# Operand sums of a two-level Strassen feed-forward moved beside the projections, and attention probabilities per head pair

## The chip, the cores and the metric

The kernel runs on one core of a Trainium2 chip. TensorE multiplies matrices, VectorE, ScalarE and GpSimd (DVE, ACT and POOL in the profile) work element by element, and SyncE (SP) issues nearly all transfers, from one queue, in order. The metric is the time of one execution on the device in microseconds.

## The reference, cut to what matters

One decoder layer on 2048 tokens of width 1024: a modulated RMSNorm, a combined projection, sliding-window attention beside a state-space scan, an output projection, a second modulated RMSNorm and a gated feed-forward of width 2816.

```python
h = modulate(rmsnorm(x, norm1_w), shift1, scale1)
x = x + gate1 * hybrid_mixer(h, ...)      # attention and SSD heads, then @ w_out
h = modulate(rmsnorm(x, norm2_w), shift2, scale2)
x = x + gate2 * swiglu(h, w_gate_up, w_down)
return rmsnorm(x, final_norm_w)

# in the attention, per head, over a band of 256 keys
m = maximum(max(scores), sink)
p = exp(scores - m)
probs = p / (sum(p) + exp(sink - m))
# swiglu
g, u = split(h @ w_gate_up, 2)
out = (silu(g) * u) @ w_down
```

## The kernel before

**Tiling.** Tokens are held in four blocks of 512 columns; features lie on the 128 partitions. Every f32 product is made from split operands: a rounded upper half (`hi`, written by ScalarE) and the rest (`lo`, by VectorE or GpSimd), three products per pair (`mm3`, lines 275 to 277; `product`, lines 918 to 920).

**Stages.** Blocks 0 to 3 go through norm, queries, keys and values, `convolved` (16 steps: eight column groups in two halves), and `gated` (eight steps). Attention and state-space work of earlier blocks is interleaved as "sides": after every step of the main stage `tick` (line 1224) advances the sides by a ratio, counts down entries of `pending`, and starts those that have reached zero. `norm_ahead(b, at)` (line 1266) puts the four parts of the norm of block b there: squares and their sum at once, then the root (`rstd`, a product with ones, line 290), the spread over partitions (line 319) and the modulated operands (`modulated`, lines 324 to 327) at the ticks given.

**Order of the work.** Up to line 1342 TensorE's order is the one written in the program. The other engines, and TensorE later on, are ordered by a planner that simulates the program and takes, on each engine, the earliest traced instruction that is ready. SP's queue gets its order in the same way.

**The feed-forward's first product.** Two blocks of tokens make a group, s = 0 for blocks 0 and 1, s = 1 for blocks 2 and 3. The gate and up products of a group use a Strassen-Winograd form (`quad`, 22 of them per group): seven products in place of eight, with sums of operands. With h[i, j] the half i of the features of block j of the group, the operands are b11 and b21 (from block one alone), b22 (from block two alone), t1 = h01 - h00, t3 = h11 - h01, t2 = h00 + t3 and t4 = h10 - t2, each made for four K tiles, shifts added. `scaled` (lines 862 to 870) loads a tile of the residual from DRAM (`mid`, L868) and multiplies it by the norm's scale and root (L869). `shifted` (L874, L875) and `kept` (L879, L880) write the two halves of an operand. `operands_first` makes b11 and b21, `operands_between` t1, `operands_last` b22, t3, t2, t4. For s = 0 the first two run beside `convolved(3)` (lines 1333 to 1338), the last is emitted in one piece after the first product of the first quad (line 1356). For s = 1 `last_operands` (line 1391) runs as a side of `down(1)`, between first, last after it. A first quad takes its products K tile by K tile (`fresh`).

**Attention.** Per tile of 128 tokens, `scores` runs twice (four heads each), then `probabilities` for all eight heads: eight exponentials with sums (L650), the denominators (L651 to L653), eight scalings (L656). The transposes and products with the values of the tile before (`held`, lines 558 to 566; `transposed`, L662 to L666; `values`) come after each pair.

**Buffers and tail.** `tmp` has eight tiles (256 KB each) for all uses; `staged` four (z, q and kv on their way to DRAM); `extra` gives working tiles to the state-space side of blocks 0 and 1. In `down(3)` the last norm's root uses ScalarE's square root (`quick_root`, L307); line 1001 issues a square root with no operand from the data ahead of it.

## Time and profile before

| | us |
|---|---|
| median of three runs | 2375.27 |
| lowest, highest | 2369.06, 2376.70 |
| the profiled execution | 2371.23 |
| its span, first to last instruction | 2369.5 |
| TensorE busy | 2245.6 |
| VectorE busy | 1463.7 |
| GpSimd busy | 1240.4 |
| ScalarE busy | 962.0 |

A span stands on the time line from the first instruction on. An engine's busy time counts its compute instructions; idle time in front of an instruction is put down to what released it, and a line like "PE d L290 <- POOL acc L285" reads: TensorE, writing d at line 290, waited for GpSimd's write of acc at line 285. PEclk is the granted clock of TensorE as a share of 2.4 GHz.

### The profile page before, as it was taken

The numbers are of one execution on the slowest core, as the hardware profiler recorded it, in microseconds if no ns is written. First come the engines' busy times: TensorE is split into PE (matmuls) and PEld (weight loads), VectorE is DVE, ScalarE is ACT, GpSimd is POOL, SyncE is SP. The second block draws the span as 40 slices with busy tenths as digits, with TensorE's granted clock in tenths as the row PEclk, the third lists the DMA queues.
The fourth block names the chain that finished last, engine by engine and source line by source line (L and its number), as shares of the span: only waits on it lengthen the run. The fifth ranks groups of instructions, "written<-read, shape, count | busy, mean of one in ns | idle before, by whom it ended". The sixth has DMA issues, their size and how long they took to land.

```text
span 2369.5 us, 33207 instructions
## 1 busy us (share of the span) xinstructions
PE 2245.6 (95%) x11292; PEld 1861.3 (79%) x11292; DVE 1463.7 (62%) x2549; ACT 962.0 (41%) x2002; POOL 1240.4 (52%) x1227
## 2 busy tenths in 40 slices
PE   6788989999999899999999999988999999999998
PEld 5578788788878688887888788866788888888787
DVE  8887975673465865667755453499654445454544
ACT  4454543654255545333333332334333333343332
POOL 2756433453222764787875432437766666653441
PEclk9899999999999899999999999999999999999999
DMA  8898977677885322332234865575322222263452
GB/s 294 287 332 302 308 252 245 229 249 261 279 266 158 117 82 78 103 107 87 92 98 150 268 214 177 165 260 161 135 92 81 85 83 82 81 221 103 130 181 63
DMA packets 249065, 412.22 MB, mean 174 GB/s; under 512 B 22464, under 2 KB 68544, under 8 KB 248896
## 3 DMA queue, kind: packets, MB, share of 16 engines
q1 hardware_dynamic: 248320, 409.58, 52.8%
q8 instruction: 89, 1.46, 0.3%
q14 instruction: 80, 0.66, 0.1%
q10 hardware_dynamic: 576, 0.52, 0.1%
HBM read 315.58 MB, written 94.44 MB: 173 GB/s over the span
## 4 chain that ended last, share of the span: by engine, by line
PE 43%; DVE 4%; DMA 1%; issue 1%; POOL 1%; ACT 0%; SPq 0%; DVEq 0%; POOLq 0%; ACTq 0%
PE d L275 5%; PE d L276 5%; PE d L277 5%; PE d L918 5%; PE d L920 5%; PE d L919 5%; PE am L920 1%; PE am L918 1%; PE am L919 1%; PE sm L920 1%; PE sm L918 1%; PE sm L919 1%; DVE t L869 1%; PE am L275 1%; PE am L277 1%
## 5 line engine op out<-in xcount | busy, mean ns | idle before, releaser
L919 PE MATMUL d<-b,w 128*128 128x512 f32 x924 | 367.5, 398 | 3.0 <-POOL b L880 2.9
L918 PE MATMUL d<-b,w 128*128 128x512 f32 x924 | 366.2, 400 | 3.6 <-ACT b L879 1.6
L920 PE MATMUL d<-b,w 128*128 128x512 f32 x924 | 366.1, 398 | 2.8 <-DVE w L850 2.8
L849 ACT ACTIVATE w<-raw 128x512 fp32r<-128x512 f32 x308 | 193.1, 630 | 432.6 <-PE d L277 218.2
L275 PE MATMUL d<-a,w 128*128 128x512 f32 (+1 forms) x720 | 282.9, 396 | 17.4 <-DVE x L1029 13.3
L276 PE MATMUL d<-a,w 128*128 128x512 f32 (+1 forms) x720 | 280.6, 390 | 1.9 <-DVE a L844 1.9
L277 PE MATMUL d<-a,w 128*128 128x512 f32 (+1 forms) x720 | 282.0, 392 | 0.0
L850 DVE TENSOR_TENSOR w<-raw,w 128x512 fp32r<-128x512 f32 x220 | 211.2, 962 | 73.1 <-ACT w L849 69.7
L850 POOL TENSOR_TENSOR w<-raw,w 128x512 fp32r<-128x512 f32 x88 | 121.4, 1380 | 221.8 <-ACT w L849 203.1
L1029 DVE SCALAR_TENSOR_TENSOR x<-d,mod,x 128x512 f32<-128x512 f32 (+1 forms) x182 | 131.0, 724 | 170.9 <-PE d L277 168.0
L919 PEld LDWEIGHTS d<-b,w 128*128 128x128 f32 x924 | 175.0, 189 | 43.2 <-POOL b L880 4.3
L918 PEld LDWEIGHTS d<-b,w 128*128 128x128 f32 x924 | 174.4, 189 | 43.4 <-ACT b L879 2.6
L920 PEld LDWEIGHTS d<-b,w 128*128 128x128 f32 x924 | 174.4, 189 | 43.4 <-DVE w L850 3.3
L850 POOL TENSOR_TENSOR w<-s,w 128x512 fp32r<-128x512 f32 x132 | 190.9, 1448 | 23.2 <-ACT w L849 22.3
L849 ACT ACTIVATE w<-s 128x512 fp32r<-128x512 f32 x176 | 111.0, 632 | 210.5 <-PE d L920 157.0
L275 PE MATMUL d<-w,hl 128*128 128x256 f32 (+1 forms) x592 | 175.7, 297 | 4.4 <-ACT hl L326 2.3
L275 PEld LDWEIGHTS d<-a,w 128*128 128x128 f32 x720 | 135.9, 189 | 53.9 <-DVE x L1029 9.1
L276 PE MATMUL d<-w,hl 128*128 128x256 f32 (+1 forms) x592 | 170.9, 289 | 0.0
L277 PE MATMUL d<-w,hl 128*128 128x256 f32 (+1 forms) x592 | 170.6, 288 | 0.0
L276 PEld LDWEIGHTS d<-a,w 128*128 128x128 f32 x720 | 136.3, 189 | 33.5 <-DVE a L844 3.1
L277 PEld LDWEIGHTS d<-a,w 128*128 128x128 f32 x720 | 135.7, 188 | 30.8 <-issue 0.5
L934 POOL TENSOR_TENSOR s<-raw,s 128x512 f32<-128x512 f32 x44 | 58.6, 1331 | 186.6 <-DVE w L850 112.6
(387 smaller groups left out, 5457.3 us busy)
## 6 DMA issues: line engine op xcount, KB each, us to landing
raw<-in_wgu_dram SPq DMA_DIRECT2D x176, 256.0 KB, 2.7
raw<-in_wd_dram SPq DMA_DIRECT2D x176, 256.0 KB, 2.7
w<-w_x SPq DMA_DIRECT2D x48, 512.0 KB, 5.3
w<-w_o SPq DMA_DIRECT2D x48, 512.0 KB, 4.6
act<-t SPq DMA_DIRECT2D x88, 256.0 KB, 2.1
t<-act SPq DMA_DIRECT2D x88, 256.0 KB, 4.5
t<-in_xT_dram SPq DMA_DIRECT2D x80, 256.0 KB, 4.4
aw<-in_wada_dram SPq DMA_DIRECT2D x64, 256.0 KB, 4.2
```

The costliest lines, as they stand in the source:

```text
L275: nc.tensor.matmul(out, ahi, bhi, start=first, stop=False)
L276: nc.tensor.matmul(out, ahi, blo, start=False, stop=False)
L277: mm3.last = nc.tensor.matmul(out, alo, bhi, start=False, stop=last)
L849: nc.scalar.activation(hi, x, AF.Copy)
L850: eng.tensor_tensor(lo, x, hi.bitcast(F32), ALU.subtract)
L869: nc.vector.scalar_tensor_tensor(x, x, scl2[:, d:d + 1], bc[j], ALU.mult, ALU.mult)
L918: nc.tensor.matmul(out, ahi, bhi, start=first and k == 0, stop=False, skip_group_check=True)
L919: nc.tensor.matmul(out, ahi, blo, start=False, stop=False, skip_group_check=True)
L920: mm3.last = nc.tensor.matmul(out, alo, bhi, start=False, stop=k == 3, skip_group_check=True)
L934: nc.gpsimd.tensor_tensor(s4, a12, s2, ALU.subtract)
L1029: nc.vector.scalar_tensor_tensor(x, ps, gate2[:, c:c + 1], x, ALU.mult, ALU.add)
```

## The change

It has five parts. First, for s = 0 the sums t3, t2, t4 and the scaled h11 are computed beside `convolved(3)` and `gated(3)` (`sums_ahead`), stored to DRAM (`raw_d`) and loaded again after the first quad's first product (`operands_kept`), where only the halves are written; the lower half of t2 goes to VectorE, those of t3 and t4 stay on GpSimd. `operands_first` and `operands_between` move to earlier steps. Second, `probabilities` runs once per pair, for four heads. Third, for s = 1 the separate pass for t1 is gone, t1 comes out of the pass of `operands_last`, with one more yield. Fourth, the ticks of the norms of blocks 1 and 3 are later. Fifth, the square root without data is tied to an operand of the fourth group of `down(3)`; `staged` has six tiles, the extra working tiles are nine.

```diff
-    common, extra = tiles(sb, M1, M2, M4), tiles(xp, 3, 10, 4)
+    common, extra = tiles(sb, M1, M2, M4), tiles(xp, 3, 9, 4)
...
-        return small([P, 256], "so", 4, pool=ip)
+        return small([P, 256], "so", 6, pool=ip)
...
-                if pair_of:
-                    probabilities(st, sms, slots)
-                    if t + 1 < NT:
-                        nxt = load(t + 1)
+                probabilities(st, sms, slots, pair_of)
+                if pair_of and t + 1 < NT:
+                    nxt = load(t + 1)
...
-    def probabilities(st, sms, slots):
-        mx, nm, den, es = (st[:, i, :] for i in range(4))
+    def probabilities(st, sms, slots, pair_of):
+        heads = range(4 * pair_of, 4 * pair_of + 4)
+        mx, nm, den, es = (st[:, i, 4 * pair_of:4 * pair_of + 4] for i in range(4))
...
+    raw_d = [[dr.tile([P, T], F32, name=f"raw_{n}{k}") for n in ("b22", "t3", "t2", "t4")] for k in range(4)]
+
+    def sums_ahead(s, bc):
+
+        for k in range(4):
+            h = scaled(s, k, bc, ((1, 1), (0, 1), (0, 0), (1, 0)))
+            t3, t2, t4 = h[0, 1], h[0, 0], h[1, 0]
+            nc.vector.scalar_tensor_tensor(t3, h[1, 1], dsh[:, k:k + 1], h[0, 1], ALU.add, ALU.subtract)
+            nc.vector.scalar_tensor_tensor(t2, h[0, 0], shift_of(k, 0), t3, ALU.add, ALU.add)
+            nc.vector.scalar_tensor_tensor(t4, h[1, 0], shift_of(k, 1), t2, ALU.add, ALU.subtract)
+            for to, x in zip(raw_d[k], (h[1, 1], t3, t2, t4)):
+                nc.sync.dma_start(to, x)
+            yield
+
+    def operands_kept(ops):
+        for k in range(4):
+            got = []
+            for n, src in zip(("t2", "t3", "b22", "t4"), (2, 1, 0, 3)):
+                x = tmp()
+                scaled.last = nc.sync.dma_start(x, raw_d[k][src])
+                got.append((n, x))
+            for n, x in got:
+                if n == "b22":
+                    shifted(ops[n][k], x, shift_of(k, 1))
+                else:
+                    kept(ops[n][k], x, nc.vector if n == "t2" else nc.gpsimd)
...
-            t3, t2, t4 = h[0, 1], h[0, 0], h[1, 0]
+            t3, t1, t2, t4 = h[1, 1], h[0, 1], h[0, 0], h[1, 0]
             nc.vector.scalar_tensor_tensor(t3, h[1, 1], dsh[:, k:k + 1], h[0, 1], ALU.add, ALU.subtract)
             kept(ops["t3"][k], t3)
+            nc.vector.tensor_tensor(t1, h[0, 1], h[0, 0], ALU.subtract)
+            kept(ops["t1"][k], t1)
+            yield
...
-            nc.scalar.activation(small([P, 1], "first_root", 1, pool=x_pool), ident[:, 0:1], AF.Sqrt)
+            first_root = small([P, 1], "first_root", 1, pool=x_pool)
...
+                    if at_group == 3 and c == 0 and b == NB - 1:
+                        nc.scalar.activation(first_root, act[0][0][:, 0:1].bitcast(F32), AF.Sqrt, scale=0.0)
...
-                nxt = norm_ahead(1, (11, 14, 15))
+                nxt = norm_ahead(1, (12, 18, 19))
...
-        nxt = norm_ahead(3, (6, 12, 22))
+        nxt = norm_ahead(3, (10, 15, 22))
...
-            if i == 8:
+            if i == 6:
+                drain(firsts)
                 bcs.append(spread(y_of[1], bc=side_bank(3)))
                 firsts = operands_between(0, ops, bcs)
-            if i % 2:
+            if i == 12:
+                drain(firsts)
+                firsts = sums_ahead(0, bcs)
+            if i < 4 or 6 <= i < 14 and i % 2 == 0 or i >= 12 and i % 2:
+                next(firsts, None)
+        for i in beside(gated(3, h), 0.5):
+            if i in (1, 3):
                 next(firsts, None)
         drain(firsts)
-        run(gated(3, h), 0.5)
...
-    drain(operands_last(0, ops, bcs))
+    operands_kept(ops)
...
-        yield from operands_between(1, ops, bcs)
         yield from operands_last(1, ops, bcs)
```

## Rows read from the trace of the kernel before

**Rows 1.** The page: span, and busy time of TensorE with its share and instructions.
```profile
span 2369.5 us, 33207 instructions
...
PE 2245.6 (95%) x11292; PEld 1861.3 (79%) x11292; DVE 1463.7 (62%) x2549; ACT 962.0 (41%) x2002; POOL 1240.4 (52%) x1227
```

**Rows 2.** Stretches of 20 us: length, busy PE, PEld, DVE, ACT, POOL, PEclk, DMA, GB/s.
```profile
420.00:440.00 20.00, 14.74 (x72) 12.15 (x71) 13.07 (x38) 7.30 (x16) 11.50 (x23) 0.83 0.50 172
...
760.00:780.00 20.00, 15.58 (x86) 12.46 (x85) 15.49 (x23) 13.80 (x33) 13.17 (x10) 1.00 0.48 150
780.00:800.00 20.00, 13.93 (x59) 10.65 (x58) 19.40 (x31) 8.31 (x16) 11.33 (x9) 0.73 0.57 166
800.00:820.00 20.00, 18.22 (x83) 13.81 (x81) 17.59 (x29) 13.59 (x39) 15.42 (x11) 0.93 0.22 80
```

**Rows 3.** What TensorE waited for, whole run: us in total, times, longest us.
```profile
PE d L275 <- DVE x L1029: 13.3, 9, 3.9
PE am L275 <- DVE m L666: 11.8, 6, 3.5
...
PE d L290 <- POOL acc L285: 5.3, 1, 5.3
...
PE d L319 <- DVE t L317: 2.8, 1, 2.8
```

**Rows 4.** Stretches of 5 us around the root of block 3.
```profile
425.00:430.00 5.00, 1.19 (x6) 1.20 (x6) 2.78 (x3) 2.53 (x4) 4.58 (x11) 0.75 0.48 154
430.00:435.00 5.00, 5.00 (x20) 4.47 (x20) 3.42 (x10) 1.54 (x3) 3.16 (x7) 0.57 0.03 11
```

**Rows 5.** VectorE's group of 1535 to 1650 us, and stretches there.
```profile
L869 DVE SCALAR_TENSOR_TENSOR t<-t,scl,bc 128x512 f32<-128x512 f32 x8 | 5.7, 738 | 0.0
...
1580.00:1600.00 20.00, 16.06 (x65) 11.64 (x64) 20.00 (x29) 6.56 (x12) 9.50 (x7) 1.00 0.71 221
...
1640.00:1660.00 20.00, 15.62 (x61) 12.12 (x60) 16.11 (x18) 9.19 (x16) 15.37 (x11) 0.91 0.36 101
```

**Rows 6.** Groups of VectorE, 760 to 812 us, by form: busy us, mean ns, idle before.
```profile
L869 DVE SCALAR_TENSOR_TENSOR t<-t,scl,sm 128x512 f32<-128x512 f32 x8 | 5.9, 736 | 0.5 <-DMA t<-mid 0.5
L869 DVE SCALAR_TENSOR_TENSOR t<-t,scl,st 128x512 f32<-128x512 f32 x8 | 5.8, 740 | 3.6 <-DMA t<-mid 3.5
L907 DVE SCALAR_TENSOR_TENSOR t<-t,mod 128x512 f32<-128x512 f32 x4 | 4.6, 1148 | 0.0
```

**Rows 7.** Groups of GpSimd, 755 to 812 us, by form.
```profile
L880 POOL TENSOR_TENSOR b<-t,b 128x512 fp32r<-128x512 f32 x12 | 17.0, 1422 | 6.8 <-ACT b L879 6.8
...
L616 POOL TENSOR_TENSOR v_ring<-m,v_ring 128x128 fp32r<-128x128 f32 x2 | 0.9, 464 | 25.9 <-ACT v_ring L615 25.9
```

**Rows 8.** Timeline of GpSimd, 755 to 812 us: start, us, what.
```profile
766.54 1.30 POOL L928 TENSOR_TENSOR s<-raw 128x512 f32<-128x512 f32 x1
...
808.83 2.51 POOL L880 TENSOR_TENSOR b<-t,b 128x512 fp32r<-128x512 f32 x2
```

**Rows 9.** Stretches of 20 us beside conv and gates of block 3.
```profile
720.00:740.00 20.00, 20.00 (x124) 17.34 (x124) 8.96 (x19) 8.74 (x17) 7.07 (x11) 0.97 0.63 178
740.00:760.00 20.00, 20.00 (x175) 19.73 (x175) 6.64 (x19) 8.10 (x25) 0.21 (x1) 1.00 0.22 80
```

**Rows 10.** The page: a store of one tile, KB, median us from issue to landing.
```profile
act<-t SPq DMA_DIRECT2D x88, 256.0 KB, 2.1
```

**Rows 11.** ScalarE's timeline behind eight exponentials; TensorE's wait in 180 to 200.
```profile
179.78 0.36 ACT L665 ACTIVATE m<-am 128x256 fp32r<-128x256 f32 x1
...
PE am L275 <- DVE m L666: 2.0, 1, 2.0
```

**Rows 12.** Timeline of the tail.
```profile
2352.98 1.28 ACT L307 ACT_TABLE_LOAD   x1
...
2354.51 0.17 DVE L308 RECIPROCAL qr<-qr 128x2 f32<-128x2 f32 x1 [2.02 <-ACT qr L307]
```

**Rows 13.** What SP's queue waited for, 640 to 830 us.
```profile
SPq L498 <- DVE so L497: 19.0, 5, 10.4
```

More of the change, by code (lines that the diff above doesn't have):

```diff
@@ L641, in scores @@
         return sms
-    def probabilities(st, sms, slots):
-        mx, nm, den, es = (st[:, i, :] for i in range(4))
+    def probabilities(st, sms, slots, pair_of):
+        heads = range(4 * pair_of, 4 * pair_of + 4)
+        mx, nm, den, es = (st[:, i, 4 * pair_of:4 * pair_of + 4] for i in range(4))
         ns = len(slots)
         nc.vector.tensor_scalar(nm, mx, -1.0, None, ALU.mult)
-        nc.vector.tensor_tensor(es, sinks, nm, ALU.add)
-        for i in range(8):
+        nc.vector.tensor_tensor(es, sinks[:, 4 * pair_of:4 * pair_of + 4], nm, ALU.add)
+        for e, i in enumerate(heads):
             sm = sms[i // 2][:, i % 2, 0:ns, :]
-            nc.scalar.activation(sm, sm, AF.Exp, bias=nm[:, i:i + 1], accum_out=den[:, i:i + 1])
+            nc.scalar.activation(sm, sm, AF.Exp, bias=nm[:, e:e + 1], accum_out=den[:, e:e + 1])
         nc.scalar.activation(es, es, AF.Exp)
@@ L653, in probabilities @@
         nc.vector.reciprocal(den, den)
-        for i in range(8):
+        for e, i in enumerate(heads):
             sm = sms[i // 2][:, i % 2, 0:ns, :]
-            nc.scalar.activation(sm, sm, AF.Copy, scale=den[:, i:i + 1])
+            nc.scalar.activation(sm, sm, AF.Copy, scale=den[:, e:e + 1])
     def transposed(sm, pT, ns, at):
```

## Prediction

> **What bounds the kernel now.** I read the page's busy rows first: TensorE is busy for 2245.6 of 2369.5 us [rows 1]. So 123.9 us is all the idle time that any edit can give back, beside time in which the engine runs at the lower of its two clock levels. The matrix work itself is left alone by the change: no product is added or dropped. The question is therefore which idle gaps of TensorE lie where the change acts, and what ends each of them. I took three views for that. The stretches of 20 us show where the gaps are: 5.3 us in 420 to 440, and 4.4, 6.1 and 1.8 us in the three stretches from 760 to 820 [rows 2]. The list of what TensorE waited for names who ends them [rows 3]. The groups and the timeline of the releasing engine then tell what that engine was doing instead.
>
> Three places come out of this. **Around 428 us** TensorE waits 5.3 us for GpSimd's sum of squares (L285), for the norm of block 3 [rows 3]. The granted clock then stands at 0.75 and 0.57 in the next two stretches of 5 us [rows 4], which means part of the time at 1.2 instead of 2.4 GHz; at full rate that is (0.25 + 0.43) x 5 = 3.4 us more. **From 760 to 820 us**, at the first quad, the operands b22, t3, t2, t4 are made while TensorE needs them. It sits idle for 12.3 us, and the clock is 0.73 and 0.93 in the last two stretches [rows 2], another (0.27 + 0.07) x 20 = 6.8 us at full rate: 19.1 us lost. **From 1580 to 1660 us** VectorE is busy for all 20 us of a stretch while TensorE is idle for 3.9 and 4.4 us of the first and the last of them [rows 5]; there VectorE is the bound, and TensorE waits for its L1029 (13.3 us in all) [rows 3].
>
> **The change part by part.**
>
> *First group, second tokens' sums made earlier.* In 760 to 812 us VectorE runs 8 + 8 scalings (L869, 5.9 + 5.8 us) and four each of L905, L907, L909 and L875 [rows 6]; with L907 at 4.6 us for its four and the others near it, that is about 29 us in 52. After, only four L875 (b22) and four lower halves of t2 are left there, 4 x 0.7 to 4 x 1.15 us each: 6 to 9 us, so VectorE is no longer the last. GpSimd loses 4 of its 12 lower halves (17.0 us, 1.42 us each) [rows 7], and is next: it does nothing until 766.5 us since it is held for 25.9 us at L616 (the values' lower half, which waits for ScalarE), and only then starts the first quad's weight sums at L928 [rows 7, 8]. Those are seven operations of 1.3 to 1.75 us, near 10.7 us; eight lower halves of 1.42 are 11.4. So GpSimd can be done at 766.5 + 22.1 = 788.6, where before its last ones ended at 811.3 [rows 8]. That lifts more than TensorE has lost; what stays is the gap up to 780 us, 4.4 us, which hangs on L616 and L928 and not on the operands, and the waits of the attention's products in between (L666). Of the 19.1 us I take **12 us as gain**; the ends are 4 (GpSimd's lower halves come as late as the weight sums let them) and 19.
>
> *What this costs beside conv and gates.* The sums are the same 28 VectorE operations, 16 x 0.74 + 12 x 0.74 to 1.15 [rows 6] = 20.7 to 25.6 us. The loops place them from conv step 12 of 16 on, which by TensorE's pace is about 715 to 745 us. VectorE is idle there for 11.0 us of 720 to 740 and 13.4 us of 740 to 760 [rows 9], 24.4 in all: they just fit. Moving the first and second operand passes to earlier steps adds nothing to that sum. On SP the 16 loads move up, and 16 stores to DRAM and 16 loads back come in; a store of 256 KB lands in 2.1 us [rows 10], so the last is down well before 765. Queued behind those stores on SP are the gates' weight loads, the gates' own stores and the first quad's weights; TensorE's conv banks are queued behind VectorE's evacuation (L485), four of them deep. I take **5 us as cost**; the ends are 0 (it fits) and 12 (VectorE's lateness, one more attention wait as at L666, 1.7 to 3.5 us each [rows 3], and a late bank).
>
> The trace also bears on one rule of the skill. L869, whose second operand lies in PSUM, takes 736 to 740 ns, and L907, with both in SBUF, 1148 ns beside a busy GpSimd [rows 6]. The Trainium skill ("SBUF — State Buffer", "SBUF: two separate sides") says that VectorE with two SBUF inputs and GpSimd exclude each other for whole instructions. By that rule the twelve two-input sums also meet the conv's GpSimd adds in their new place.
>
> *Norm of block 3, from tick 6 to 10 (and 12 to 15).* Four steps of conv later GpSimd's last add is long done (TensorE is busy again from 430 on [rows 4]); nothing else moves but the products in front. The 5.3 us wait goes and with it the low clock: 8.7 us at most. **8 us gain**, ends 3 and 8.7.
>
> *Norm of block 1, 11 to 12, 14 to 18, 15 to 19.* The spread's wait for VectorE (L319, 2.8 us [rows 3]) goes, since six ticks and not three lie between root and spread. But the operands of block 1 are made four ticks later, and queries(1) follows five ticks on. **2 us gain**; ends 4 gained and 4 lost (queries wait as long for an operand as the spread did, and a bit more).
>
> *Probabilities per pair.* Now eight exponentials stand in one piece on ScalarE, and the transposed copy L665 comes right behind the last, and TensorE's L275 waits 2.0 us for L666 behind it [rows 11]. After, four stand there. L666 is waited for 11.8 us in its largest row [rows 3]; I take a third of it for waits behind such a block. Added are 4 small VectorE operations and one exponential per token tile, sixteen times, some 0.2 us each, spread over the whole attention; behind them on VectorE wait the evacuations. The trace shows no half-length block, so I bound it: **4 us gain**, ends 9 gained (all of these waits and the clock behind some) and 5 lost (pair 0's exponentials come before the first transposes, where none stood).
>
> *Second group in one pass.* Eight loads and eight scalings L869 fall away, 8 x 0.74 = 5.9 us of VectorE [rows 5], in a stretch that VectorE sets. t1 comes with its K tile and no longer first; nothing needs it before the quads, which start after the stretch. **6 us gain**, ends 1 (GpSimd with its sixteen lower halves is next) and 9 (a lower clock that goes too).
>
> *The root's table.* The preload of down(3) needs no data and can run ahead of the last quads' tanh, which undoes it; a table load of 1.28 us stands at 2352.98 on the tail, where VectorE waits 2.02 us for the root [rows 12]. Tied to the third group's operand, the load moves under the down products. The other half's columns run on meanwhile, so **1 us gain**, ends 0 and 2.
>
> *Buffers.* One working tile fewer for the state-space part of blocks 0 and 1, two more staging tiles: no wait in the list is put down to them. **0**, ends 0 and 4 lost.
>
> **Sum:** -12 + 5 - 8 - 2 - 4 - 6 - 1 = -28 us. Against the profiled execution, 2371.2 us (a span of 2369.5 and 1.7 around it), that is 2343. The median of the three runs, 2375.3, lies 4.0 above the profiled one, so I forecast **2347 us**. The single ends, taken as independent (root of the sum of squares), give 11 us below and 17 above: 2336 to 2364.
>
> **The rivals.**
>
> *GpSimd holds the first quad.* For it: L616's 25.9 us, and the weight sums that can only begin then [rows 7, 8]; against: it has a third less to do. The gain of 12 becomes 4: **2355**.
>
> *Sums made too late to be of use.* If the stores come out after the gates, the read-back waits for them, and the first quad starves as now. For it: stores on SP waited up to 10.4 us for L497 in this place [rows 13]; against: 24 us of idle VectorE. Gain 0, cost 5 as before: 2371.2 + 5 - 8 - 2 - 4 - 6 - 1 + 4.0 = **2359**.
>
> *Two-input sums blocked by GpSimd.* The twelve at twice L869's time cost 12 x 0.74 = 8.9 us more, which no longer fits under 24.4 us: 20.7 + 8.9 = 29.6, and the cost goes from 5 to about 10: **2352**. This is what the rule above would make of it; against it in the rows, the four of L907 come to 1148 ns on average and not to twice 740, beside a GpSimd that is busier than it is during conv. The Trainium skill's page "SBUF — State Buffer" is the one that states that lock.
>
> *Slower: SP's order.* Four batches of four stores each stand in front of the gates' and the first quad's weight loads and hold the queue until VectorE is through. With 10.4 us per batch, the longest wait of a store seen there [rows 13], that is 41.6 us. Six weight tiles of 24 products are ahead, at 20 us for 175 products [rows 9] 16.5 us of cover, so TensorE stands for 25 us in four gaps, each with 3.4 us at the lower clock behind it as at 430 [rows 4]: 39 us. The first quad gains nothing, and 2371.2 - 8 - 2 - 4 - 6 - 1 + 39 is 2389, with the 4.0 **2393**. It makes the kernel measurably slower once the queue is held for more than about 31 us. Against it: TensorE is busy throughout from 720 to 760 although that wait of 10.4 us ends near there [rows 9].
>
> **How the numbers follow.** Forecast 0.52, GpSimd at the first quad 0.20, blocked sums 0.10, sums too late 0.10, SP's order 0.08. The range from 2333 to 2366 holds the forecast's own and the three milder rivals. A measurement of this kernel can tell some 0.3%, 7 us: faster is below 2368, slower above 2382. Of the first four nearly all lie below 2368: 0.82 faster; 0.10 within; 0.08 slower, the last rival.
>
> **What would show it.** Right: no wait of L290 for L285 near 430; the waits of L918 to L920 for L880 near 780 to 810 gone, and the first quad done before 805; VectorE busier in 715 to 760 without new gaps; 24 scalings L869 beside down(1) where there are 32 now; no table load in the last 20 us. Wrong: a stall of TensorE between 715 and 760, SP waiting on the new stores, queries(1) waiting for its operands near 175, or VectorE still busy for whole stretches after 1640.

## Result and the profile of the changed kernel

| | before | changed |
|---|---|---|
| median of the runs, us | 2375.98 (2369.06 to 2378.8, 4 runs) | 2353.14 (2350.19 to 2355.18, 4 runs) |
| the profiled execution, us | 2371.23 | 2354.35 |

The ratio is 0.9907, 95% interval 0.9883 to 0.9932: less than one per cent, but clear of no change. It is 22.8 us less between the medians, 16.9 us less between the two profiled executions. The profile of before lies 4.8 us under its median and that of the changed kernel 1.2 us over; single executions lie up to 5 us off their median below, too.

The page of the changed kernel: span, then busy time of each engine. TensorE's 2245.6 of [rows 1] are 2239.7 here, in a span that is 16.9 us shorter: its idle time fell from 123.9 to 112.9 us, and the same number of matmuls took 5.9 us less; the granted clock was 0.983 on average, where it was 0.980.

```profile
span 2352.6 us, 33306 instructions
...
PE 2239.7 (95%) x11292; PEld 1853.7 (79%) x11292; DVE 1472.6 (63%) x2609; ACT 963.6 (41%) x2016; POOL 1234.1 (52%) x1223
```

What TensorE waited for in the whole run of the changed kernel, as in [rows 3] (evacuation L1029 is L1060 here). The wait for GpSimd's L285 is gone and that for the evacuation has fallen from 13.3 to 5.0 us. That for L844, the lower half of a stored activation, has grown from 1.9 to 5.7 us, and 4.1 us for L327, an operand of block 1, are new.

```profile
PE am L275 <- DVE m L666: 7.6, 5, 3.8
PE am L276 <- DVE m L666: 6.4, 7, 2.1
PE d L276 <- DVE a L844: 5.7, 3, 3.6
PE d L275 <- DVE x L1060: 5.0, 5, 2.5
...
PE d L277 <- DVE hl L327: 4.1, 2, 3.8
```

Stretches of 20 us of the changed kernel, columns as in [rows 2]: the root of block 3, conv and gates of block 3, and the first quad.

```profile
420.00:440.00 20.00, 19.92 (x113) 16.36 (x111) 13.25 (x29) 13.47 (x34) 14.16 (x26) 1.00 0.61 197
440.00:460.00 20.00, 17.82 (x95) 14.30 (x94) 18.25 (x36) 14.93 (x32) 9.02 (x11) 1.00 0.78 258
...
715.00:735.00 20.00, 20.00 (x134) 17.70 (x134) 18.11 (x36) 12.61 (x29) 5.93 (x7) 1.00 1.01 373
735.00:755.00 20.00, 20.00 (x168) 19.39 (x167) 17.19 (x37) 9.92 (x28) 1.68 (x1) 1.00 0.76 271
```

At the root TensorE is busy for 19.92 us instead of 14.74, at full clock [rows 2]. Beside conv and gates VectorE is busy for 18 and 17 us of 20 and TensorE for all of them: the sums went in without a gap.

**Where the time went, by stage.** From the timelines I took the first TensorE product of each stage's own matrix work (queries, conv, gates, projections, quads, downs) and so the length of each stage. The start of conv of block 0 and the stages that are not in this table differ by 0.7 us or less each, 1.9 in all. A: gates of block 0 to the start of block 2's conv. B: conv of block 2. C: second out projection and conv of block 3. D: the first group's quads. E: down of blocks 0 and 1. F: down of blocks 2 and 3 without the last halves (those last 16.8 us in every kernel). The further rows are the experiments, with the ratio of their times to those of before.

| kernel | ratio, 95% interval | median | A | B | C | D | E | F |
|---|---|---|---|---|---|---|---|---|
| before | 1 | 2375.98 | 253.5 | 73.6 | 117.7 | 581.9 | 327.5 | 246.0 |
| changed | 0.9907 (0.9883 to 0.9932) | 2353.14 | 253.8 | 68.8 | 113.2 | 573.3 | 326.8 | 245.2 |
| u_norm1 | 0.9917 (0.9904 to 0.9929) | 2351.95 | 251.0 | 68.5 | 114.8 | 572.0 | 326.7 | 245.2 |
| u_norm3 | 0.9926 (0.9914 to 0.9937) | 2355.08 | 253.8 | 74.0 | 114.8 | 572.7 | 327.4 | 246.5 |
| u_onepass | 0.9925 (0.9913 to 0.9936) | 2355.84 | 253.3 | 67.3 | 115.6 | 571.5 | 328.7 | 245.4 |
| u_sums | 0.9932 (0.9916 to 0.9948) | 2357.35 | 252.9 | 70.0 | 112.8 | 582.1 | 327.1 | 244.5 |
| u_prob | 0.9899 (0.9886 to 0.9913) | 2350.78 | 262.8 | 67.7 | 118.2 | 561.0 | 325.9 | 247.7 |
| v_mid | 0.9913 (0.9900 to 0.9927) | 2354.87 | 257.2 | 68.9 | 114.5 | 571.5 | 326.2 | 245.8 |
| v_acts | 0.9889 (0.9873 to 0.9904) | 2348.91 | 252.0 | 68.6 | 113.1 | 573.6 | 329.9 | 240.5 |
| v_both | 0.9896 (0.9881 to 0.9910) | 2349.49 | 255.9 | 68.6 | 114.7 | 569.7 | 326.6 | 240.6 |
| w_mix | 0.9853 (0.9835 to 0.9870) | 2336.82 | 251.7 | 68.4 | 115.3 | 557.7 | 327.1 | 245.5 |
| w_best | 0.9838 (0.9825 to 0.9852) | 2334.24 | 253.0 | 69.9 | 113.0 | 559.1 | 327.3 | 241.2 |
| w_best1 | 0.9837 (0.9823 to 0.9852) | 2334.41 | 254.8 | 68.5 | 116.1 | 559.3 | 325.2 | 241.2 |
| x_pair | 0.9947 (0.9931 to 0.9963) | 2362.82 | 244.8 | 75.1 | 114.0 | 583.7 | 332.2 | 247.4 |

The table carries its own yardstick. Where an edit has no line in a stage, the stage still moves a little, since the planner orders the engines anew: the seven kernels with shorter pieces and the changed ticks have A between 251.7 and 253.8, all kernels with shorter pieces in blocks 0 to 2 have C between 112.8 and 116.1. Each stage is read from one execution besides. Two kernels with the same lines in a stage differ by 3.8 us in A (u_norm1 and w_best1) and by 4.7 in E (before and x_pair). So a difference under 5 us in one stage of one kernel says nothing by itself; one that all kernels with an edit have and none without it does.

Between before and changed, the gain lies in B (-4.8), C (-4.5) and D (-8.6); A, which holds the norm of block 1, gave nothing, and E only 0.7.

### The profile page after: what moved, and what is told of

Read it like the earlier page. It is cut to its first block, busy times and chain, and to the rows that moved or that the text cites. A ratio compares the mean times of both kernels' runs of the same rounds, so it can differ in the third digit from the quotient of the medians.

```text
span 2352.6 us, 33306 instructions
## 1 busy us (share of the span) xinstructions
PE 2239.7 (95%) x11292; PEld 1853.7 (79%) x11292; DVE 1472.6 (63%) x2609; ACT 963.6 (41%) x2016; POOL 1234.1 (52%) x1223
## 5 line engine op out<-in xcount | busy, mean ns | idle before, releaser
L850 DVE TENSOR_TENSOR w<-raw,w 128x512 fp32r<-128x512 f32 x220 | 207.6, 945 | 62.1 <-ACT w L849 58.8
L850 POOL TENSOR_TENSOR w<-raw,w 128x512 fp32r<-128x512 f32 x88 | 121.0, 1375 | 228.4 <-ACT w L849 212.8
L1060 DVE SCALAR_TENSOR_TENSOR x<-d,mod,x 128x512 f32<-128x512 f32 (+1 forms) x182 | 131.1, 724 | 173.6 <-PE d L277 169.9
L850 POOL TENSOR_TENSOR w<-s,w 128x512 fp32r<-128x512 f32 x132 | 187.2, 1420 | 31.2 <-ACT w L849 30.7
```

The source lines that it names most:

```text
L850: eng.tensor_tensor(lo, x, hi.bitcast(F32), ALU.subtract)
L1060: nc.vector.scalar_tensor_tensor(x, ps, gate2[:, c:c + 1], x, ALU.mult, ALU.add)
```

## Experiments

**One part undone at a time.** Each of the first five kernels is the changed one with a single part put back.

*u_norm1, the norm of block 1 on its former ticks.*

```
-                nxt = norm_ahead(1, (12, 18, 19))
+                nxt = norm_ahead(1, (11, 14, 15))
```

> The changed kernel with one part undone: the norm of block 1 is back on ticks 11, 14, 15. Theory (operands made too late): the first matrix work of block 1, its queries, lost 9.2 us in the changed kernel (the next part began 9.5 us later than before, where the part ahead of it began 0.3 later), because TensorE waited 4.1 + 1.8 us for the halves of block 1's operands (L327, L326) and then ran at a granted clock of 0.83 and 0.74. With the ticks back this goes: the keys and values of block 1 start at about 213 to 214 instead of 222.7 us, the waits for L326 and L327 are gone there, a wait of 2 to 3 us for the spread (L319) is back, and the time is 5 to 9 us below the changed kernel's 2353, some 2344 to 2348, ratio to before 0.987 to 0.989. Rival 1 (the loss is that of the probabilities per pair, which are new in the same stretch): nothing moves, 2351 to 2355, and the start stays near 222. Rival 2 (the forecast's own step, a gain of 2 from the later ticks): 2355, slower than the changed kernel.

Measured: no change in time (0.9917). Inside the stretch much moved. TensorE's timeline in the changed kernel shows the wait for an operand of block 1 in the queries, and that of this kernel the wait for the spread:

```profile
207.86 0.58 PE L277 MATMUL d<-w,hl 128*128 128x256 f32 x1 [3.81 <-DVE hl L327]
```

```profile
135.07 2.08 PE L319 MATMUL d<-t,ones 128*128 128x512 f32 x2 [4.88 <-DVE t L317]
```

With the former ticks the part from the gates of block 0 to the start of block 1's keys and values took 68.7 us instead of 76.2, but conv of block 1 took 77.7 instead of 70.9. What TensorE lost at the queries, it got back in the conv behind them; that side work had caught up meanwhile is likely, but no row shows it. The first theory had the stall right and its price wrong.

*u_norm3, the norm of block 3 on its former ticks.*

```
-        nxt = norm_ahead(3, (10, 15, 22))
+        nxt = norm_ahead(3, (6, 12, 22))
```

> The changed kernel with one part undone: the norm of block 3 is back on ticks 6, 12, 22. Theory (the forecast's step, confirmed in size by the stage that it lies in): the root of block 3 again stands in front of TensorE's conv products before GpSimd's sum of squares is done, the wait of L290 for L285 is back with about 5 us and the low clock behind it with up to 3; conv of block 2 takes 4.7 to 8.7 us more, and the time is 2358 to 2362, ratio to before 0.992 to 0.995. Rival (the wait only showed what the state-space work beside it holds up anyway): the wait moves to another row of the same stretch, and the time stays within 2 us of 2353.

Measured: B takes 74.0 us in place of 68.8; the three kernels with the former ticks (before, x_pair and this one) have 73.6 to 75.1, the eleven others 67.3 to 70.0. The ratio rises by 0.0019 (4.5 us), which by itself lies within the intervals. What TensorE waited for in 400 to 475 us of this kernel, first row, then the stretch: the wait of [rows 3] and the low clock of [rows 2] are back.

```profile
PE d L290 <- POOL acc L285: 4.0, 1, 4.0
...
420.00:440.00 20.00, 15.80 (x77) 12.91 (x76) 15.45 (x40) 10.13 (x22) 13.14 (x24) 0.83 0.39 129
```

*u_onepass, the second group's t1 in a pass of its own.*

```
     def last_operands():
         ...
-        yield from operands_last(1, ops, bcs)
+        yield from operands_between(1, ops, bcs)
+        yield from operands_last_apart(1, ops, bcs)
```

where `operands_last_apart` is the last pass of the kernel before.

> The changed kernel with one part undone: the second group's t1 is again made in a pass of its own ahead of the others, with 8 more loads and 8 more scalings on VectorE (32 instead of 24 beside the down products). Theory A (the forecast: VectorE sets this stretch, so 8 scalings of 0.74 us are 6 us): down of blocks 0 and 1 together take about 6 us more and the time is 2359. Theory B (by the two traces: these stages gained only 0.7 us, because the loads of the stored activations of the next group stand later on the queue and VectorE's lower halves of them come late): 0 to 2 us more, 2353 to 2355. Under B the waits of TensorE for L844 and for ScalarE's copy of the activations (3.6 and 1.9 us at 1600 to 1610) are smaller or gone, and those for VectorE's evacuation (L1060 in the changed kernel) are about 13 us again instead of 5.

Measured: E takes 1.9 us more, which is within the scatter; theory B. VectorE's work was saved as forecast. Stage E of the changed kernel, then of this one, columns as in [rows 2]:

```profile
1326.40:1653.20 326.80, 313.99 (x1329) 249.80 (x1330) 202.30 (x292) 117.36 (x194) 152.96 (x108) 0.98 0.59 189
```

```profile
1322.60:1651.30 328.70, 314.02 (x1329) 249.70 (x1330) 206.98 (x300) 116.48 (x194) 149.83 (x107) 0.98 0.59 194
```

VectorE is busy for 4.7 us more; its instructions overlap a little, and their durations come to 222.1 us here and 216.3 in the changed kernel, 5.8 more. What TensorE waited for in 1326 to 1670 us, first of the changed kernel, then of this one (L1073, L1037 are its L1060, L1024):

```profile
PE d L276 <- DVE a L844: 5.7, 3, 3.6
PE d L275 <- DVE x L1060: 5.0, 5, 2.5
PE d L275 <- ACT a L1024: 2.1, 2, 1.9
```

```profile
PE d L275 <- DVE x L1073: 12.6, 9, 3.8
PE d L275 <- ACT a L1037: 1.4, 1, 1.4
PE d L276 <- DVE a L844: 0.4, 1, 0.4
```

12.8 us against 14.4: the wait for the evacuation shrank by 7.6, and 6.0 of these came back as waits for the activations.

*u_sums, the first group's sums at the first quad.*

```
             if i == 12:
                 drain(firsts)
-                firsts = sums_ahead(0, bcs)
+                firsts = iter(())
     ...
-    operands_kept(ops)
+    drain(operands_last_apart(0, ops, bcs))
```

where the last pass is that of the kernel before.

> The changed kernel with one part undone: the second tokens' sums of the first group are again made at the first quad, from loads and scalings there, with nothing kept in DRAM (the earlier steps of the first two passes stay). Theory (the forecast's step, of the size the traces show): conv and gates of block 3 lose nothing by it, the first quads lose 8 to 12 us again (waits for L880 from 780 to 812 and the lower clock), so 2361 to 2365, ratio to before 0.994 to 0.996. Rival 1 (the gain at the first quad is that of the probabilities per pair and of the shifted attention work, not of the sums): 2352 to 2356. Rival 2 (the 3.7 us that conv of block 3 gained came from the sums' new place or the other passes' earlier steps, and go with them): a further 4 us, some 2366. The blocked two-input sums: the groups of the three sums beside conv in the changed kernel against those beside the first quad here tell how long each takes beside a busy and an idle GpSimd.

This puts the lower halves of t2 back on GpSimd, too, so the run does not tell the sums from that. Measured: D takes 8.8 us more, C 0.4 less; 6 us by the ratios, whose intervals overlap. D is 582.1 here and 569.7 to 573.6 in the seven kernels with shorter pieces and early sums. Stretches of 40 us from the first quad on, of this kernel, of the changed one and of w_mix (below), columns as in [rows 2]:

```profile
751.10:791.10 40.00, 31.81 (x144) 24.72 (x143) 35.08 (x53) 21.13 (x43) 27.11 (x21) 0.84 0.58 185
791.10:831.10 40.00, 37.43 (x174) 29.42 (x172) 27.37 (x56) 24.45 (x63) 25.98 (x21) 0.95 0.19 60
```

```profile
753.10:793.10 40.00, 36.95 (x200) 29.34 (x199) 31.80 (x41) 26.97 (x55) 35.88 (x26) 1.00 0.64 198
793.10:833.10 40.00, 36.52 (x176) 28.76 (x175) 28.48 (x53) 22.10 (x61) 23.89 (x18) 1.00 0.28 93
...
1073.10:1113.10 40.00, 37.17 (x161) 30.32 (x160) 26.60 (x32) 12.20 (x27) 31.20 (x29) 0.91 0.26 86
```

```profile
752.40:792.40 40.00, 36.94 (x201) 29.29 (x200) 32.22 (x41) 27.39 (x55) 35.84 (x26) 1.00 0.64 198
792.40:832.40 40.00, 40.00 (x194) 32.01 (x193) 27.36 (x55) 20.00 (x51) 27.02 (x20) 1.00 0.30 93
...
1072.40:1112.40 40.00, 40.00 (x185) 32.84 (x184) 27.38 (x34) 16.19 (x35) 32.69 (x35) 1.00 0.36 112
```

Idle time plus the share of the clock that is missing, over the first 80 us: 8.2 + 2.6 + 0.16 x 40 + 0.05 x 40 = 19.2 us with the sums at the first quad, 3.0 + 3.5 = 6.5 us in the changed kernel, 3.1 in w_mix. In these 80 us the early sums are worth 12.7 us, of which 8.8 are left at the end of D. (A little is counted twice, where the clock was low while TensorE was idle.)

The same sums in their two places, groups of VectorE by form: in the changed kernel from 700 to 760 us, then in this one from 750 to 815.

```profile
L908 DVE SCALAR_TENSOR_TENSOR t<-t,mod 128x512 f32<-128x512 f32 x4 | 4.0, 1002 | 0.0
...
L909 DVE SCALAR_TENSOR_TENSOR t<-t,mod 128x512 f32<-128x512 f32 x4 | 3.3, 826 | 0.0
L907 DVE SCALAR_TENSOR_TENSOR t<-t,dsh 128x512 f32<-128x512 f32 x4 | 3.0, 745 | 0.0
```

```profile
L953 DVE SCALAR_TENSOR_TENSOR t<-t,mod 128x512 f32<-128x512 f32 x4 | 5.2, 1309 | 0.0
L949 DVE SCALAR_TENSOR_TENSOR t<-t,dsh 128x512 f32<-128x512 f32 x4 | 4.8, 1188 | 0.0
L951 DVE SCALAR_TENSOR_TENSOR t<-t,mod 128x512 f32<-128x512 f32 x4 | 4.4, 1092 | 0.0
```

10.3 us for the twelve beside conv and a GpSimd with 7.6 us of work in 40 (715 to 755), 14.4 at the first quad beside one with 27.1 in 40. Beside conv ten of the twelve took 0.74 to 0.75 us, two 1.07 and 1.78. The rival of the blocked sums falls: they became cheaper by the move.

*u_prob, probabilities for all eight heads in one piece.*

```
-                probabilities(st, sms, slots, pair_of)
-                if pair_of and t + 1 < NT:
-                    nxt = load(t + 1)
+                if pair_of:
+                    probabilities(st, sms, slots)
+                    if t + 1 < NT:
+                        nxt = load(t + 1)
...
```

> The changed kernel with one part undone: the probabilities of a token tile are again made for all eight heads in one piece behind the second pair's scores. Theory A (the forecast's step): the shorter pieces were worth about 4 us, spread over the attention of all blocks: waits for L666 are again 11 us and more in all, and 2357. Theory B (they are what made conv of block 3 shorter: in the changed kernel, and still with the sums of the first group moved back to the first quad, that stage takes 113 us where it took 117.7 before, and nothing else of the change lies in it but the earlier steps of two operand passes): the stage is 117 to 118 again, and the time 2357 to 2361. Theory C (that gain is that of the earlier steps of the operand passes): the stage stays at 113, and the time is 2351 to 2355. In the stretch from the gates of block 0 to the keys and values of block 2, 145 to 400 us, A and B expect a few us more, C none.

Measured: the time is that of the changed kernel (0.9899), and yet this is the part that moves most. A takes 9.0 us more and C 5.0, as theory B has it, though its time of 2357 to 2361 did not come; D takes 12.3 us less, which no theory had. The shorter pieces help beside queries and conv and cost as much beside the quads. Stage A of the changed kernel, then of this one, and what TensorE waited for at L666 in the whole run of this one:

```profile
146.50:400.30 253.80, 229.01 (x1597) 210.26 (x1597) 197.50 (x493) 116.50 (x298) 122.62 (x177) 0.95 0.85 281
```

```profile
144.90:407.70 262.80, 232.81 (x1598) 214.03 (x1597) 187.95 (x472) 114.02 (x287) 122.12 (x177) 0.92 0.82 272
```

```profile
PE am L276 <- DVE m L666: 6.5, 7, 2.9
PE am L275 <- DVE m L666: 6.4, 3, 3.4
```

Of the 9.0 us 5.2 are idle time of TensorE (30.0 for 24.8); the rest is time in which it is busy, at a granted clock of 0.92 in place of 0.95. The waits for L666 are not the main cause: they come to 12.9 us with eight heads and 14.0 with the shorter pieces.

**Follow-ups.** Can the norm of block 1 and the second group be had for more?

*v_mid and v_acts, and both in v_both.*

```
-                nxt = norm_ahead(1, (12, 18, 19))
+                nxt = norm_ahead(1, (11, 15, 16))
```

```
-                    if c == 3:
+                    if c == 1:
                         next_tokens()
```

(the second in both loops of `down`).

> The changed kernel with the norm of block 1 on ticks 11, 15, 16, between the former 11, 14, 15 and the changed 12, 18, 19. With the former ticks the queries of block 1 took 7.5 us less than in the changed kernel, but conv of block 1 took 6.8 us more, and the stretch from the gates of block 0 to the start of block 2's conv 251.0 where it took 253.8. Theory A (that stretch is set by VectorE's and ScalarE's work beside it, and a wait of TensorE in one part of it is given back in the next): 250 to 253 again whatever the ticks, and a time of 2349 to 2353. Theory B (each wait counts by itself: the wait of 4.9 us for the spread at tick 14 goes, and the operands still come in time): 246 to 248, and a time of 2345 to 2348.

> The changed kernel with one line more: the loads of the next group's activations beside the down products are issued behind the second chunk of output features and not behind the fourth, in all four blocks. Theory (the 6 us that VectorE was to give back in down of block 1 went into a new wait, because these loads stood on the queue at 1598 to 1602 us, about 15 us later than in the kernel before against its own start of the stage): the waits for L844 and for the copies of the activations at 1600 to 1610 (5.7 and 2.1 us) go, down of blocks 0 and 1 takes 321 to 324 us in place of 326.8, and the time is 2348 to 2351. Rival (VectorE sets the stretch with what it has to do, whatever the order: only the name of the last releaser changes): 326 to 327, waits for VectorE's evacuation (L1060) of 9 to 13 us in place of 5, and 2353.

> The norm of block 1 on ticks 11, 15, 16 and the loads of the next group's activations behind the second chunk, both together in the changed kernel. If the two act in places of their own, the time is the sum of what each gives alone: 2344 to 2348 by the theories that expect a gain of each, 2349 to 2353 by the rivals.

Measured: v_mid has A at 257.2 us, v_both at 255.9, where theory A had 250 to 253 and theory B 246 to 248. Theory B falls; no pair of ticks beats another by more than the scatter, as theory A says, but this pair may be some 3 us worse. With v_acts E does not fall but stands at 329.9, and what TensorE waited for in 1322 to 1656 us is again the evacuation:

```profile
PE d L275 <- DVE x L1060: 11.5, 7, 2.9
PE am L319 <- DVE t L317: 2.1, 1, 2.1
PE d L276 <- DVE a L844: 1.5, 1, 1.5
```

So the late loads were not the cause; VectorE has to do all of this work in that stretch, and only the name of the instruction for which TensorE waits last changes. The rival holds. Unlooked for, F fell by 4.7 us: there the wait for ScalarE's copy of the activations (L1024, 2.6 us in the changed kernel) went with the low clock, and nothing took its place. The four kernels with the earlier loads there have F at 240.5 to 241.2, the ten others at 244.5 to 247.7.

*w_mix, w_best, w_best1: shorter pieces for blocks 0 to 2 only.*

```
-                probabilities(st, sms, slots, pair_of)
+                if b < 3:
+                    probabilities(st, sms, slots, pair_of)
+                elif pair_of:
+                    probabilities_of_all(st, sms, slots)
```

w_best adds the earlier loads (second chunk) in blocks 2 and 3 alone, w_best1 also the former ticks of block 1's norm.

> The changed kernel, with the probabilities per pair for blocks 0 to 2 and for all eight heads in one piece for block 3, whose attention runs beside the first quads. With eight heads everywhere the stretch from the gates of block 0 to conv of block 2 took 9.0 us more than in the changed kernel and conv of block 3 took 5.0 more, but the first group's quads took 561.0 in place of 573.3. Theory A (the shorter pieces help where attention stands beside queries, keys, values and conv, and hurt beside the quads): both gains are kept, the quads take 560 to 565, and the time is 2339 to 2345. Theory B (of the 12.3 us, 6.2 hang on one wait for L708 of the state-space work of block 2 near 1080 and 2.4 on one for L253 near 1230, neither of them attention's; where they fall is the luck of the planned order, and the rest comes from the first quad starting 10 us later): the quads take 569 to 574, and the time stays at 2350 to 2354. The wait of L779 for L708 (2.7 us) is gone under A and may stay under B.

> As the mixed one (probabilities per pair for blocks 0 to 2, all eight heads at once for block 3), and the loads of the next group's activations behind the second chunk in down of blocks 2 and 3 alone, where they gave 4.7 us without a wait in its place (in blocks 0 and 1 the same edit gave none, since VectorE sets that stretch). Expected: down of blocks 2 and 3 takes 240.5 us in place of 245.2, whatever the quads do; the time is 4 to 5 us below that of the mixed one: 2335 to 2341 if the mixed one is at 2339 to 2345, 2345 to 2349 if it is at 2350 to 2354.

> As the one with both edits, and the norm of block 1 back on ticks 11, 14, 15. With the probabilities per pair the stretch from the gates of block 0 to conv of block 2 took 251.0 us on these ticks and 253.8 on the later ones. If the three act in places of their own, it is 2 to 3 us below the one without this edit. Rival: the planned order of the work behind it comes out otherwise, and what is gained at 400 us is gone by 760.

Measured: theory A. A and C keep their gain, and D falls to 557.7 us; 2336.82, 16 us below the changed kernel and clear of its interval. With the loads it is 2334.24; their own 2.6 us lie within the intervals, and stage F shows them (241.2 for 245.5). The former ticks change nothing (2334.41).

Where D lost 12.7 of its 15.6 us in the changed kernel shows in the stretches above and in its waits from 750 to 1330 us; the rest I can't place.

```profile
PE sm L779 <- DVE m L708: 2.7, 1, 2.7
PE am L584 <- DVE ast L637: 2.6, 1, 2.6
...
PE am L275 <- ACT mo L253: 1.2, 1, 1.2
```

3.5 us lie in the second 40 us, where the transposes of block 3's next keys (L584) wait for VectorE to finish the scores (L637): that is attention's own. 2.8 us of idle time and 0.09 x 40 = 3.6 at the low clock hang on L708, and 2.8 us of idle time lie between 1193 and 1273, the longest piece of it at the out projection's L253; both belong to other work than attention. From the quads on TensorE's order is the planner's too, and in w_mix 25 quad products stand between the second decay product (L704) and L779's counterpart, 18 in the changed kernel. So a part of the gain is the planner's order and goes with any edit; but it came out so in all four kernels with eight heads in block 3 whose sums are made early (557.7 to 561.0), and in none of the seven with shorter pieces (569.7 to 573.6).

*x_pair, the same form of the probabilities alone in the kernel before* (the diff of w_mix, put on the kernel before).

> The kernel before with one part of the change alone, in the form that did best: probabilities per pair for blocks 0 to 2, all eight heads at once for block 3; all else as before, the norms' former ticks too. Theory (the part acts by itself, and the four kernels with either form and either ticks of block 1's norm add up): the stretch from the gates of block 0 to conv of block 2 takes 251 us in place of 253.5, since on the former ticks the shorter pieces are worth 2.5 and not the 9 that they are worth on the later ones; the stage from the second out projection to the gates of block 3 takes 113 in place of 117.7; the first group's quads stay near 582, with the wait of L779 for L708 that stood there before; in all 7 us, 2364 to 2367 against 2371 to 2374 of before, ratio 0.996 to 0.998. Rival (the two gains hang on the other parts, the shifted operand passes and the third block's norm): within 0.2% of before, and the two stages as before. If the quads take some 12 us less as well, eight heads in block 3 are not what mattered there.

Measured: 2362.82, ratio 0.9947: 12.6 us, near twice what was expected. C is 114.0; A is 244.8, 8.7 less and not 2.5. D stays at 583.7. In the profiles only 5.1 us show, since that of before lies 4.7 us under the median of this comparison and this one 3.3 over.

With this row the two parts can be crossed in D. While the sums are made at the first quad, the form of block 3's probabilities makes no difference: 581.9 and 583.7 with eight heads (before, x_pair), 582.1 with the shorter pieces (u_sums). With the early sums D is 557.7 to 561.0 with eight heads and 569.7 to 573.6 with the shorter pieces. The other parts of the change have no line in D. So moving the sums is worth some 21 us or more there by itself, and the shorter pieces took 12 of it back.

With this kernel A can be taken apart. Shorter pieces are worth 8.7 us on the former ticks and former buffers, and 9.0 on the new ones (u_prob against changed): the same. So what else lies in A, the ticks and the two buffer numbers, cost 9 us: 253.8 against 244.8, 262.8 against 253.5. The ticks alone are worth nothing beyond the scatter with the new buffers (251.0 and 254.8 against 251.7 to 253.8). That leaves 6 to 10 us on one working tile less and two staging tiles more. This is an inference from six kernels; the buffers alone were not tried, and no row of a wait names them.

## Why the forecast was right, and where its steps were not

The forecast was 2347 with 2333 to 2366 and the chance on faster; it came out at 2353, 22.8 below instead of 28. The mechanism held where the profile had shown a wait with an end: the first quad and the root of block 3. Half of the other terms were wrong, and that the sum came so close is luck: they cancelled. Added up by the runs, the shorter pieces gave some 14 us (A and C), the early sums behind them 9 (D), block 3's norm 5 and the second group about 1, and 6 to 10 were likely lost on the buffers.

Of the signs named, the right ones came. The last product of the first quad starts 30.9 us after the first one, at 784, where it was 51.5 us; 24 scalings are left beside down(1). Of the wrong ones the wait of block 1's queries for an operand came (at 207.9), and SP did wait on the new stores, for 6.0 us in all and without a gap of TensorE.

- **First group, -12 with ends 4 and 19.** Right in its mechanism: by the reckoning above, 19.8 us lost in the first 80 us became 6.5. The forecast had GpSimd's last lower half end 28.4 us after the first quad's start; it ends 29.1 us after it (L880 at 780.91, 1.28 us long; the quad starts at 753.1), where it was 51.1. That it fits so well is luck in part: GpSimd began its weight sums 2.9 us earlier against the quad than forecast (L959 at 756.45) and took 3.6 us longer. TensorE's waits for L880 fell to 0.3 us. Stage D gave 8.6, since further back in the quads 9.4 us are lost where it was 7.1, and 2.4 us I can't place. The crossed kernels show why the term looks so right: with eight heads in block 3 the same move gives some 21 us, above its end of 19, and the shorter pieces took the rest. The two stretches of the kernel before:

```profile
760.20:800.20 40.00, 29.51 (x142) 23.12 (x141) 35.09 (x53) 22.11 (x50) 24.50 (x18) 0.86 0.53 159
800.20:840.20 40.00, 37.48 (x175) 29.20 (x173) 31.33 (x51) 21.37 (x53) 33.40 (x25) 0.97 0.26 91
```

- **Cost beside conv and gates, +5 with ends 0 and 12.** It fits: 0.4 us in C between u_sums and changed, which is its lower end. Part of the error was to take twelve two-input sums at up to 1.15 us; their three groups took 0.75 to 1.00 on average. The rival of SP's order fell too: the longest waits there for L908 and L869 were 3.4 and 2.6 us in all, though a store landed only after 5.2 us where 2.1 had been read off [rows 10].
- **Norm of block 3, -8 with ends 3 and 8.7.** Right in kind, oversized: 4.8 to 5.2 us. The wait and the low clock went, but the next stretch, 440 to 460, now has 2.2 us of idle time: VectorE's L593 comes last there (1.7 us). And the 3.4 us for the clock hold some idle time twice: in 425 to 430, one of the two stretches, TensorE is idle for 3.8 us of 5 [rows 4].
- **Norm of block 1, -2, between 4 gained and 4 lost.** Nothing. The wait for the spread went (L319, 2.8 us [rows 3]) and that for L327 came (4.1 us), as its end of 4 lost had it; the step that failed was to add up either of them at all in a stretch where TensorE's waits are given back.
- **Probabilities per pair, -4 with ends -9 and +5.** The largest term, and split by place: some 9 us gained in A and 4 to 5 in C, which is above its end, and 12 lost in D. The step that failed was to size it by the largest row of one wait (L666), which the shorter pieces did not lessen, and to spread it evenly over the whole attention. Its own sentence on the cost, that pair 0's exponentials come before the first transposes, pointed to the loss without a place.
- **Second group, -6 with ends 1 and 9.** 0.7 to 1.9 us. VectorE did save 5.8; the sentence that VectorE sets that stretch was right, but so was its reverse: what TensorE no longer waited for the evacuation, it waited for the copies and lower halves of activations.
- **Root's table, -1.** The load left the tail, where ScalarE's timeline of the changed kernel has none and VectorE waits 0.59 us instead of 2.02 [rows 12]:

```profile
2335.68 0.19 ACT L307 ACTIVATE qr<-qr 128x2 f32<-128x2 f32 x1
2335.90 0.17 DVE L308 RECIPROCAL qr<-qr 128x2 f32<-128x2 f32 x1 [0.59 <-ACT qr L307]
```

  The last halves take 16.8 us all the same, and from the last product to the end it is 12.1 us where it was 11.8: the second half covers the first half's root. Nothing gained, the lower end. (It is tied to the fourth group, as the diff has it, not to the third.)
- **Buffers, 0 with 4 lost.** Likely 6 to 10 lost, as worked out above; not shown alone.

## What to carry to other kernels

Move operand work away from the place where the consumer starts, and keep the results in DRAM if they don't fit: at the first quad it paid 12.7 us, of which a later stage can take some back, and it cost nothing where VectorE had 24 us to spare. A reorder of side work must be judged stage by stage and switched per stage: one form of the probabilities was worth 14 us in front of the quads and minus 12 beside them, and its total hid both. Cross two parts before calling either's term right: the loss of the one showed only where the other had cleared the stage. Where an engine is busy for whole stretches, taking away a wait or one of its operations names the next one on the same engine; a part of its work has to leave the stretch.

## What the runs showed of the hardware

A VectorE instruction on SBUF alone can stand still for the rest of a GpSimd instruction. VectorE's and GpSimd's timelines, of the changed kernel and then of w_mix, around the same two small conversions (L531, L532):

```profile
1073.99 1.74 POOL L850 TENSOR_TENSOR w<-s,w 128x512 fp32r<-128x512 f32 x1
1074.50 1.26 DVE L531 CAST ahi<-t 128x32 fp32r<-128x32 f32 x1
1075.69 1.30 POOL L999 TENSOR_TENSOR t<-t 128x512 f32<-128x512 f32 x1
1075.80 1.23 DVE L532 TENSOR_TENSOR alo<-t,ahi 128x32 f32<-128x32 f32 x1
```

```profile
1053.53 0.17 DVE L531 CAST ahi<-t 128x32 fp32r<-128x32 f32 x1
...
1054.22 0.18 DVE L532 TENSOR_TENSOR alo<-t,ahi 128x32 f32<-128x32 f32 x1
```

In w_mix GpSimd had one operation of two columns beside the first of them, and none until the second was nearly done. The subtraction L532, with both inputs in SBUF, takes 0.18 us there; in the changed kernel it takes 1.23 and ends at 1077.03, 0.04 us after GpSimd's L999. The conversion L531, with one input, takes 0.17 and 1.26 us and ends at 1075.76, 0.03 us after L850.

The lower halves L844 on VectorE, with both inputs in SBUF, show the same over the changed kernel from 600 us on. 17 of them began while a GpSimd instruction ran: 16 of these ended 0.55 us after that instruction did, whatever was left of it, and took up to 1.80 us (1.37 on average for the 17). 13 began first and had GpSimd begin beside them: 0.68 us, as the 14 with none beside them (0.69). So VectorE is held up where GpSimd began first, and not where it began first itself. The evacuation L1060, with an operand in PSUM, took 0.73 to 0.75 us, 84 times beside GpSimd and 100 times without. The Trainium skill ("SBUF — State Buffer", "SBUF: two separate sides") calls this an exclusive lock for whole instructions, for VectorE with two SBUF inputs or in a two-port mode; the rows of L532, L844 and L1060 agree, and of L531 no row here tells the mode. In the forecast the price of this rival was too high for the new place, where GpSimd has little to do; at the first quad the same twelve sums took 14.4 us.
